# Seven-product matrix stages: GpSimd's sums moved to VectorE and PSUM, and another order of the products

## The chip, the cores and the metric

One core of one Trainium2 chip runs the whole program. The metric is the device time of one execution in microseconds (us); several executions are timed and the median is taken. The engines are TensorE (PE, its weight loads PEld), VectorE (DVE), ScalarE (ACT), GpSimd (POOL) and SyncE (SP), which issues most of the DMAs.

## The reference

512 tokens of width 1024, in float32, go through two programs one behind the other. The first is one block: three branches (dilated attention, a pooling mixer, a state-space scan), gated and added up, a product with `w_o`, and a feed-forward part of width 2816. The second has two layers: three branches (differential attention, retention, grouped-query attention), gated, a product with `w_out`, and an MLP of width 4096. What matters here are the products that come back to width 1024:

```
x = x + merged @ w_o[i]
x = x + conv_ffn(rmsnorm(x, ln2_g[i]), ffn_w_up[i], ffn_conv_w[i], ffn_conv_b[i], ffn_w_down[i])
...
h = h + jnp.einsum('bsd,de->bse', merged, w_out[l])
m = jnp.einsum('bsd,df->bsf', rms_norm(h, mlp_norm[l]), w_mlp_in[l])
m = jnp.square(jax.nn.relu(m))
h = h + jnp.einsum('bsf,fd->bsd', m, w_mlp_out[l])
```

## The kernel before, in words

**Every large product is split.** A float32 operand becomes a high half (ACT's copy, L294) and a low half (DVE's subtraction, L295), and each term of a product is three matmuls (high by high, high by low, low by high). `split` (L293) does that. Weights come raw in DMAs of 512 KB on SP's queue into one of RAWS buffers, and `halve` (L235) splits each 128x1024 piece into `whi` and `wlo`, of which there are HALVES buffers each. Products of the `feat` kind are lines 269 to 271, of the `tok` kind lines 280 to 282.

**`quick` (L928) is the product back to width 1024 by seven block products in place of eight.** Left side and weights are cut into 2x2 blocks. The products of sums of blocks, lines 960 to 962, are added up into the four blocks of X (pages of 128x512). It runs 14 times: once for `w_o`, three times for `ffn_w_down` (8, 8 and 6 pages of 128 features), and in each of the two layers once for `w_out` and four times for `w_mlp_out`, each time right behind the stage that makes the pages of its left side.

**`Forms` (L71) makes the sums of the left blocks.** Each time two new pages r1 and r2 are there, `make` (L85) forms r2 (products 2 and 4), r1 (products 1 and 7), s (products 5 and 6) and w (product 3) from them: three sums of 128x256 on POOL (L89 to L91), one on DVE (L92), and splits each of the four with ACT and DVE. 55 pairs of pages go this way.

**The sums of the weight blocks** are `combine` (L948): eight sums of 128x1024 per run, of which every second is POOL's:

```
def combine(out, x, y, op):
    for j, (o, a, b) in enumerate(zip(out, x, y)):
        engines[j % 2].tensor_tensor(o, a, b, op=op)
```

The products run in the order 1, 5, 3, 6, 2, 7, 4, and the weight blocks are loaded in the order b11, b12, b22, b11 again, b21. Product 1 goes to the PSUM bank pair `a`; ACT copies it out (L998) to the pages `u`, DVE adds product 6 to them (L1019, L1021), and POOL adds `u` to X eight times per run (`add_u`, L973). The other products are added from PSUM to X by DVE (`add`, L967 and L969).

**What sets the order.** Each engine works through its own list of instructions in order. A scheduler makes the lists when the program is built: it places each instruction by its sources' expected times, so that an edit in one place moves others. An instruction that waits holds up all that stand behind it on its engine. Products 1 and 5 are written with their last pair of pages (k = n - 1) left for later (L989 and below), so that matmuls on older pages stand ahead of those that need the pages made last. `gated` (L640) frees its pages `y` at its very end.

Of the kernel before, what the change touches and what calls it, by code (L numbers as in the profile page):

```python
# [12 lines left out]
AF = mybir.ActivationFunctionType  # L13
ALU = mybir.AluOpType
# [10 lines left out]
RAWS = 5  # L25
HALVES = 6
# [44 lines left out]
class Forms:  # L71
# [13 lines left out]
    def make(self, r1, r2):  # L85
        B = self.body
        g, v, c, d = B.nc.gpsimd, B.nc.vector, slice(0, 256), slice(256, 512)
        s, w = B.pgs(2, True)
        g.tensor_tensor(s.t[:, c], r1.t[:, d], r2.t[:, d], op=ALU.add)  # L89
        g.tensor_tensor(s.t[:, d], s.t[:, c], r1.t[:, c], op=ALU.subtract)  # L90
        g.tensor_tensor(w.t[:, c], r2.t[:, c], s.t[:, d], op=ALU.subtract)  # L91
        v.tensor_tensor(r1.t[:, d], r1.t[:, c], r1.t[:, d], op=ALU.subtract)  # L92
        out = []
# [24 lines left out]
class Body:  # L118
# [521 lines left out]
    def gated(self, U, wg, g0, bias, y, wy, kt, acc, first, last, perm=False):  # L640
# [8 lines left out]
        for i in range(8 + AHEAD):  # L649
# [23 lines left out]
            t = T.pop(c)  # L673
            if first:
                a = self.pg()
                acc.append(a)
                nc.vector.scalar_tensor_tensor(a.t, t.t, 1.0, py, op0=ALU.add, op1=ALU.mult)
            else:
                a = acc[c].t
                nc.vector.scalar_tensor_tensor(t.t, t.t, 1.0, py, op0=ALU.add, op1=ALU.mult)  # L680
                (nc.vector if last else nc.gpsimd).tensor_tensor(t.t if last else a, a, t.t, op=ALU.add)
# [6 lines left out]
        self.free(y)  # L688
# [239 lines left out]
    def quick(self, w, k0, kt, F, X, scale=1.0, rows=None, turn=None):  # L928
# [8 lines left out]
        engines = (nc.vector, nc.gpsimd)  # L937
# [10 lines left out]
        def combine(out, x, y, op):  # L948
            for j, (o, a, b) in enumerate(zip(out, x, y)):
                engines[j % 2].tensor_tensor(o, a, b, op=op)  # L950
# [20 lines left out]
        def add_u(t, h, u):  # L971
            x = X[t][h].t
            nc.gpsimd.tensor_tensor(x, x, u.t, op=ALU.add)  # L973

# [15 lines left out]
        u = self.pgs(2)  # L990
# [4 lines left out]
        product(5, W5, d, b=n - 1)  # L995
        product(1, W1, a, a=n - 1)
        for q in two:
            nc.scalar.activation(u[q].t, a[q], AF.Copy, scale=scale)  # L998
            add_u(q, 0, u[q])
        product(5, W5, d, a=n - 1)  # L1000
        b22 = [load(2, 2, j) for j in js]
        W3 = right(b22)
# [3 lines left out]
        combine(b12, b22, b12, ALU.subtract)  # L1006
        b11 = [load(1, 1, j) for j in js]
        combine(b11, b12, b11, ALU.add)
        W6 = right(b11)
        for q in two:  # L1010
            add(q, 1, d[q])
        b = bank()
        product(6, W6, b)
        W7 = right(b12)
        b21 = [load(2, 1, j) for j in js]
        W2 = right(b21)
        for q in two:
            if scale == 1.0:
                nc.vector.tensor_tensor(u[q].t, u[q].t, b[q], op=ALU.add)  # L1019
            else:  # L1020
                nc.vector.scalar_tensor_tensor(u[q].t, b[q], scale, u[q].t, op0=ALU.mult, op1=ALU.add)  # L1021
            add_u(q, 1, u[q])
            sums(q)
        for q in two:
            add_u(2 + q, 1, u[q])
            add_u(2 + q, 0, u[q])
        e = bank()
        product(2, W2, e)
        combine(b21, b21, b11, ALU.subtract)
        for q in two:  # L1030
            add(q, 0, e[q])
            if rows:
                xn[q] = rows(q, ss[q])
        c = bank()
        product(7, W7, c)
        W4 = right(b21)
        for q in two:
            add(2 + q, 1, c[q])
            sums(2 + q)
            if turn:  # L1040
                turn(q, xn[q])
        product(4, W4, c, more=True)
        for q in two:
            add(2 + q, 0, c[q])
            if rows:
                xn[2 + q] = rows(2 + q, ss[2 + q])
        self.free(u, F)
# [730 lines left out]
```

## Time and profile before

| what | value |
|---|---|
| median of 3 runs | 2946.03 us (2943.02 to 2946.54) |
| the profiled execution, its own time | 2942.34 us |
| span in the trace | 2940.2 us |
| mean granted TensorE clock | 0.985 |
| PE busy | 2830.1 us (96%) |
| DVE busy | 2041.5 us (69%) |
| ACT busy | 1307.2 us (44%) |
| POOL busy | 938.3 us (32%) |
| chain that ended last, by engine | PE 76%, DVE 8%, POOL 7%, DMA 4%, ACT 2%, issue 2% |

The profiled execution lies 3.7 us below the median of the runs. Its span is 2.1 us shorter than its own time. Matmuls are pipelined, so one that is shown with 0.39 us starts 0.227 us after the one before it; the distance of two starts is what counts.

### The profile page before, as it was taken

What the parts mean: (1) busy time and instruction counts of PE and PEld (TensorE: products, weight loads), DVE (VectorE), ACT (ScalarE), POOL (GpSimd) and SP (SyncE); (2) the same over time, 40 slices, a digit from 0 to 9 for tenths busy, and PEclk for the clock granted to TensorE, in tenths of its full rate; (3) what the DMA queues carried; (4) which work ended last, traced back from release to release, by engine and by line L of the source; (5) the groups of instructions that cost most, each with busy time, mean ns of one, the idle gap of its engine ahead of it and who ended that gap; (6) DMA issues with size and microseconds to landing.
All of it is one profiled execution on the core that took longest, in us unless ns stands there. A gap on an engine that the chain in (4) does not pass through costs nothing.

```text
span 2940.2 us, 36920 instructions
## 1 busy us (share of the span) xinstructions
PE 2830.1 (96%) x13639; PEld 2361.2 (80%) x13639; DVE 2041.5 (69%) x3316; ACT 1307.2 (44%) x2249; POOL 938.3 (32%) x763
## 2 busy tenths in 40 slices
PE   8999999998999979999999899999999999989999
PEld 7888887887877868888787777787888887778777
DVE  4345477757778786856776787777765766877776
ACT  4344243334444445553464444444554455444443
POOL 0001105314132244211632344345321432534444
PEclk9999999999999989999999999999999999999999
DMA  7243331324242432222222332344222222323341
GB/s 217 82 126 105 100 97 55 88 77 151 74 142 72 133 112 87 88 75 73 73 69 68 118 112 88 101 130 149 84 65 89 64 67 61 122 83 115 115 129 65
DMA packets 225655, 288.20 MB, mean 98 GB/s; under 512 B 17769, under 2 KB 155331, under 8 KB 225475
## 3 DMA queue, kind: packets, MB, share of 16 engines
q1 hardware_dynamic: 212288, 272.77, 30.4%
q10 hardware_dynamic: 13187, 13.08, 1.5%
q8 instruction: 107, 1.75, 0.2%
q14 instruction: 73, 0.60, 0.1%
HBM read 276.30 MB, written 11.67 MB: 98 GB/s over the span
## 4 chain that ended last, share of the span: by engine, by line
PE 76%; DVE 8%; POOL 7%; DMA 4%; ACT 2%; issue 2%; ACTq 0%; SPq 0%; POOLq 0%; DVEq 0%
PE mm L270 14%; PE mm L269 14%; PE mm L271 14%; PE mm L280 4%; PE mm L281 4%; PE mm L282 4%; PE ax L960 4%; PE ax L961 4%; PE ax L962 4%; PE ax L301 3%; DVE wlo L295 3%; POOL raw L950 2%; DMA raw<-in_w_mlp_out_dram 2%; POOL pg L89 1%; DVE pg L295 1%
## 5 line engine op out<-in xcount | busy, mean ns | idle before, releaser
L295 DVE TENSOR_TENSOR wlo<-raw,whi 128x1024 fp32r<-128x1024 f32 (+3 forms) x554 | 730.3, 1325 | 276.6 <-ACT whi L294 269.1
L294 ACT CAST whi<-raw 128x1024 fp32r<-128x1024 f32 (+3 forms) x554 | 565.4, 1031 | 591.3 <-PE mm L270 318.0
L270 PE MATMUL mm<-ul,whi 128*128 128x512 f32 (+1 forms) x1792 | 689.2, 385 | 5.7 <-DVE ul L295 5.7
L269 PE MATMUL mm<-uh,whi 128*128 128x512 f32 (+1 forms) x1792 | 690.8, 387 | 2.0 <-ACT uh L294 2.0
L271 PE MATMUL mm<-uh,wlo 128*128 128x512 f32 (+1 forms) x1792 | 687.4, 384 | 0.0
L270 PEld LDWEIGHTS mm<-ul,whi 128*128 128x128 f32 x1792 | 340.7, 190 | 71.1 <-DVE ul L295 7.0
L269 PEld LDWEIGHTS mm<-uh,whi 128*128 128x128 f32 x1792 | 339.8, 190 | 66.8 <-ACT uh L294 2.9
L271 PEld LDWEIGHTS mm<-uh,wlo 128*128 128x128 f32 x1792 | 340.6, 190 | 64.7 <-issue 0.6
L960 PE MATMUL ax<-whi,pg 128*128 128x512 f32 x770 | 309.6, 406 | 55.2 <-ACT pg L294 43.8
L961 PE MATMUL ax<-wlo,pg 128*128 128x512 f32 x770 | 309.2, 402 | 0.0
L962 PE MATMUL ax<-whi,pg 128*128 128x512 f32 x770 | 298.0, 398 | 0.0
L280 PE MATMUL mm<-whi,uh 128*128 128x512 f32 (+3 forms) x736 | 280.5, 381 | 1.5 <-ACT uh L294 1.5
L281 PE MATMUL mm<-wlo,uh 128*128 128x512 f32 (+3 forms) x736 | 278.1, 378 | 0.0
L282 PE MATMUL mm<-whi,ul 128*128 128x512 f32 (+3 forms) x736 | 278.0, 378 | 0.0
L294 ACT CAST pg<-pg 128x512 fp32r<-128x512 f32 (+2 forms) x264 | 144.9, 574 | 261.8 <-DVE pg L92 66.3
L950 POOL TENSOR_TENSOR raw<-raw,raw 128x1024 f32<-128x1024 f32 (+1 forms) x56 | 159.2, 2843 | 314.7 <-DVE wlo L295 152.4
L973 POOL TENSOR_TENSOR pg<-pg,pg 128x512 f32<-128x512 f32 x112 | 209.6, 1895 | 91.0 <-ACT pg L998 48.5
L295 DVE TENSOR_TENSOR pg<-pg,pg 128x512 fp32r<-128x512 f32 (+2 forms) x264 | 198.1, 776 | 53.3 <-ACT pg L294 51.3
L960 PEld LDWEIGHTS ax<-whi,pg 128*128 128x128 f32 x770 | 149.3, 194 | 98.5 <-ACT pg L294 50.2
L89 POOL TENSOR_TENSOR pg<-pg,pg 128x256 f32<-128x256 f32 x55 | 59.1, 1075 | 421.5 <-DVE pg L1677 163.8
L301 PE MATMUL ax<-c_k_ident,pg 128*128 128x128 f32 x993 | 150.6, 279 | 33.4 <-DVE pg L1146 10.8
L962 PEld LDWEIGHTS ax<-whi,pg 128*128 128x128 f32 x770 | 149.4, 194 | 32.8 <-DVE pg L295 0.4
(264 smaller groups left out, 4387.1 us busy)
## 6 DMA issues: line engine op xcount, KB each, us to landing
raw<-in_w_in_dram SPq DMA_DIRECT2D x180, 512.0 KB, 3.7
raw<-in_w_mlp_out_dram SPq DMA_DIRECT2D x80, 512.0 KB, 3.6
raw<-in_w_mlp_in_dram SPq DMA_DIRECT2D x64, 512.0 KB, 4.3
raw<-in_ffn_w_up_dram SPq DMA_DIRECT2D x44, 512.0 KB, 3.8
raw<-in_ffn_w_down_dram SPq DMA_DIRECT2D x25, 512.0 KB, 3.5
raw<-in_w_out_dram SPq DMA_DIRECT2D x20, 512.0 KB, 3.7
raw<-in_w_branch_dram SPq DMA_DIRECT2D x16, 512.0 KB, 3.9
raw<-in_w_o_dram SPq DMA_DIRECT2D x10, 512.0 KB, 4.3
```

What stands on the lines that cost most here:

```text
L269: mm(ps, hi[:, cols], uh, start=k == 0, stop=False)
L270: mm(ps, hi[:, cols], ul, start=False, stop=False)
L271: mm(ps, lo[:, cols], uh, start=False, stop=k == nk - 1)
L280: mm(ps, uh, hi, start=k == 0, stop=False)
L281: mm(ps, uh, lo, start=False, stop=False)
L282: mm(ps, ul, hi, start=False, stop=k == n - 1)
L294: self.nc.scalar.copy(hi, src)
L295: self.nc.vector.tensor_tensor(lo, src, hi.bitcast(F32), op=ALU.subtract)
L301: self.nc.tensor.transpose(pt[:, i * P:(i + 1) * P], s, self.ident)
L960: mm(ps, uh[:, c], hi, start=not more and k == 0, stop=False, skip_group_check=more)
L961: mm(ps, uh[:, c], lo, start=False, stop=False, skip_group_check=more)
L962: mm(ps, ul[:, c], hi, start=False, stop=k == n - 1, skip_group_check=more)
```

## The change

- **`Forms.make`**: the three sums on POOL are now DVE's. The order is L89 (s's first half), then the difference inside r1 (L90, before L92), then s's second half (L91) and w (L92).
- **`combine`**: all eight sums of a run are DVE's.
- **No pages `u`**: product 6 is accumulated onto product 1 in the PSUM pair `a`, products 7 and 4 onto that; product 3 onto product 5 in the pair `d`; product 2 goes to two banks of the `mm` kind, `e`. ACT's copy (28 in all), DVE's sum with `u` (28) and `add_u` on POOL (112) are gone; DVE's adds from PSUM to X become 14 per run from 12.
- **Order**: products 1, 2, 5, 6, 3, 7, 4; weight blocks b11, b21, b12, b22, b21 again. The first two products are written without their last pair of pages. The number of matmuls and of loads stays.
- **Buffers**: 7 raw ones from 5, 5 pairs of halves from 6 (the same bytes).
- **`gated`** frees its pages `y` ahead of its last addition.

```diff
-RAWS = 5
-HALVES = 6
+RAWS = 7
+HALVES = 5
...
-        g.tensor_tensor(s.t[:, c], r1.t[:, d], r2.t[:, d], op=ALU.add)
-        g.tensor_tensor(s.t[:, d], s.t[:, c], r1.t[:, c], op=ALU.subtract)
-        g.tensor_tensor(w.t[:, c], r2.t[:, c], s.t[:, d], op=ALU.subtract)
+        v.tensor_tensor(s.t[:, c], r1.t[:, d], r2.t[:, d], op=ALU.add)
         v.tensor_tensor(r1.t[:, d], r1.t[:, c], r1.t[:, d], op=ALU.subtract)
+        v.tensor_tensor(s.t[:, d], s.t[:, c], r1.t[:, c], op=ALU.subtract)
+        v.tensor_tensor(w.t[:, c], r2.t[:, c], s.t[:, d], op=ALU.subtract)
...
             t = T.pop(c)
+            if c == 7:
+                self.free(y)
...
-        self.free(y)
...
         def combine(out, x, y, op):
-            for j, (o, a, b) in enumerate(zip(out, x, y)):
-                engines[j % 2].tensor_tensor(o, a, b, op=op)
+            for o, a, b in zip(out, x, y):
+                nc.vector.tensor_tensor(o, a, b, op=op)
...
         product(1, W1, a, b=n - 1)
-        u = self.pgs(2)
+        W2 = right([load(2, 1, j) for j in js])
+        e = [self.mm() for _ in two]
+        product(2, W2, e, b=n - 1)
+        product(1, W1, a, a=n - 1)
+        product(2, W2, e, a=n - 1)
         b12 = [load(1, 2, j) for j in js]
         combine(b11, b12, b11, ALU.subtract)
         W5 = right(b11)
         d = bank()
-        product(5, W5, d, b=n - 1)
-        product(1, W1, a, a=n - 1)
+        product(5, W5, d)
         for q in two:
-            nc.scalar.activation(u[q].t, a[q], AF.Copy, scale=scale)
-            add_u(q, 0, u[q])
-        product(5, W5, d, a=n - 1)
...
+            add(q, 0, a[q])
+        W6, W3 = [], []
+        for j in js:
+            t = load(2, 2, j)
+            combine([b11[j]], [t], [b11[j]], ALU.subtract)
+            W6 += right([b11[j]])
+            combine([b12[j]], [t], [b12[j]], ALU.subtract)
+            W3 += right([t])
+        for q in two:
+            add(q, 0, e[q])
+        product(6, W6, a, more=True)
         for q in two:
             add(2 + q, 1, d[q])
         product(3, W3, d, more=True)
+        for q in two:
+            add(q, 1, a[q])
+        W7 = right(b12)
         for q in two:
             add(q, 1, d[q])
...
+        product(7, W7, a, more=True)
+        b21 = [load(2, 1, j) for j in js]
+        combine(b21, b21, b11, ALU.subtract)
         W4 = right(b21)
         for q in two:
-            add(2 + q, 1, c[q])
+            add(2 + q, 1, a[q])
...
-        product(4, W4, c, more=True)
+        product(4, W4, a, more=True)
         for q in two:
-            add(2 + q, 0, c[q])
+            add(2 + q, 0, a[q])
```

How it moves the lists is shown at the second `w_mlp_out` run of the first layer, which the rows further below show too. Lines behind 680 have other numbers in the changed kernel: 1663 there is 1677 before, the instruction that makes a page of the MLP. In the names, `pg` are pages of 128x512, `raw` the raw weights, `whi` and `wlo` their halves, `ax` and `mm` PSUM banks. First the lists of POOL and of DVE before, from where the last pages come; the last pair r1, r2 is pg1226 and pg1228, and their sum s is pg1229:

```order
L950 TENSOR_TENSOR raw1653_15286<-raw1639_15196,raw1653_15286 128x1024
L89 TENSOR_TENSOR pg1229_15140<-pg1226_15109,pg1228_15138 128x256
L90 TENSOR_TENSOR pg1229_15140<-pg1229_15140,pg1226_15109 128x256
L91 TENSOR_TENSOR pg1230_15141<-pg1228_15138,pg1229_15140 128x256
L973 TENSOR_TENSOR pg1103_13646<-pg1103_13646,pg1237_15192 128x512
L973 TENSOR_TENSOR pg1105_13648<-pg1105_13648,pg1238_15193 128x512
```

```order
L1677 SCALAR_TENSOR_TENSOR pg1228_15138<-mm1629_15111,pg1227_15136 128x512
L295 TENSOR_TENSOR pg1234_15151<-pg1228_15138,pg1233_15150 128x512
L295 TENSOR_TENSOR wlo1655_15291<-raw1652_15284,whi1654_15290 128x1024
L92 TENSOR_TENSOR pg1226_15109<-pg1226_15109 128x256
L295 TENSOR_TENSOR pg1232_15147<-pg1226_15109,pg1231_15146 128x512
L295 TENSOR_TENSOR pg1236_15155<-pg1229_15140,pg1235_15154 128x512
L295 TENSOR_TENSOR pg1224_15067<-pg1230_15141,pg1223_15066 128x256
```

And DVE's list with the change, from the same place; r1 and r2 are pg1214 and pg1216 now, s is pg1217, and raw1644 is the second load of b21:

```order
L295 TENSOR_TENSOR wlo1625_15159<-raw1606_15076,whi1624_15158 128x1024
L1663 SCALAR_TENSOR_TENSOR pg1216_15054<-mm1605_15027,pg1215_15052 128x512
L950 TENSOR_TENSOR raw1606_15076<-raw1630_15194,raw1606_15076 128x1024
L89 TENSOR_TENSOR pg1217_15056<-pg1214_15025,pg1216_15054 128x256
L295 TENSOR_TENSOR pg1222_15067<-pg1216_15054,pg1221_15066 128x512
L950 TENSOR_TENSOR raw1644_15306<-raw1644_15306,raw1606_15076 128x1024
L90 TENSOR_TENSOR pg1214_15025<-pg1214_15025 128x256
L91 TENSOR_TENSOR pg1217_15056<-pg1217_15056,pg1214_15025 128x256
L295 TENSOR_TENSOR wlo1627_15163<-raw1607_15078,whi1626_15162 128x1024
L92 TENSOR_TENSOR pg1218_15057<-pg1216_15054,pg1217_15056 128x256
L295 TENSOR_TENSOR pg1220_15063<-pg1214_15025,pg1219_15062 128x512
```

The difference inside r1 stood behind POOL's sums (it overwrites what L89 reads), and those behind a combine of POOL's; now all stand in one list on DVE, with two combines and two halves of weights between them.

Then PE's list before and with the change, up to the first matmuls that read the pages made last (before: the high half of r1, pg1231; with the change: that of r2, pg1221, in the second piece, and that of r1, pg1219, in the third):

```order
L960 MATMUL ax1645_15209<-whi1642_15204,pg1221_15062 128x512
L961 MATMUL ax1645_15209<-wlo1643_15205,pg1221_15062 128x512
L962 MATMUL ax1645_15209<-whi1642_15204,pg1222_15063 128x512
L960 MATMUL ax1636_15172<-whi1634_15168,pg1231_15146 128x512
L961 MATMUL ax1636_15172<-wlo1635_15169,pg1231_15146 128x512
```

```order
L961 MATMUL mm1621_15121<-wlo1619_15117,pg1207_14974 128x512
L962 MATMUL mm1621_15121<-whi1618_15116,pg1208_14975 128x512
L960 MATMUL mm1620_15120<-whi1618_15116,pg1221_15066 128x512
L961 MATMUL mm1620_15120<-wlo1619_15117,pg1221_15066 128x512
L960 MATMUL mm1621_15121<-whi1618_15116,pg1221_15066 128x512
L961 MATMUL mm1621_15121<-wlo1619_15117,pg1221_15066 128x512
```

```order
L960 MATMUL ax1629_15167<-whi1624_15158,pg1183_14796 128x512
L961 MATMUL ax1629_15167<-wlo1625_15159,pg1183_14796 128x512
L962 MATMUL ax1629_15167<-whi1624_15158,pg1184_14797 128x512
L960 MATMUL ax1612_15088<-whi1610_15084,pg1219_15062 128x512
L961 MATMUL ax1612_15088<-wlo1611_15085,pg1219_15062 128x512
L960 MATMUL ax1613_15089<-whi1610_15084,pg1219_15062 128x512
```

Before, 36 matmuls of products 1 and 5 stand between the last one of the MLP and the first on r1. With the change there are 36 of products 1 and 2 ahead of the first on r2, and 52 ahead of the first on r1; the first of product 6, which adds onto the bank pair `a`, is the 73rd.

## Rows read from the trace of the kernel before

**Rows 1.** The page: busy time of the engines, and the chain that ended last

```profile
PE 2830.1 (96%) x13639; PEld 2361.2 (80%) x13639; DVE 2041.5 (69%) x3316; ACT 1307.2 (44%) x2249; POOL 938.3 (32%) x763
PE 76%; DVE 8%; POOL 7%; DMA 4%; ACT 2%; issue 2%; ACTq 0%; SPq 0%; POOLq 0%; DVEq 0%
```

**Rows 2.** Waits of PE: who for whom, us in total, times, longest us

```profile
PE ax L960 <- ACT pg L294: 43.8, 14, 4.7
PE ax L301 <- DVE pg L1146: 10.8, 1, 10.8
```

**Rows 3.** Groups by line and shape: busy us, mean ns, idle time before them

```profile
L295 DVE TENSOR_TENSOR wlo<-raw,whi 128x1024 fp32r<-128x1024 f32 x521 | 702.3, 1355 | 246.2 <-ACT whi L294 238.7 <-PE ax L301 5.2
L294 ACT CAST whi<-raw 128x1024 fp32r<-128x1024 f32 x521 | 542.7, 1052 | 552.3 <-PE mm L270 292.0 <-PE ax L962 137.1 <-POOL raw L950 49.9
L960 PE MATMUL ax<-whi,pg 128*128 128x512 f32 x770 | 309.6, 406 | 55.2 <-ACT pg L294 43.8 <-DVE pg L967 4.2 <-ACT whi L294 3.4
L973 POOL TENSOR_TENSOR pg<-pg,pg 128x512 f32<-128x512 f32 x112 | 209.6, 1895 | 91.0 <-ACT pg L998 48.5 <-DVE pg L1019 26.7 <-DVE pg L967 14.1
L950 POOL TENSOR_TENSOR raw<-raw,raw 128x1024 f32<-128x1024 f32 x52 | 153.0, 2943 | 281.8 <-DVE wlo L295 133.7 <-DMA raw<-in_w_mlp_out_dram 101.4 <-DMA raw<-in_ffn_w_down_dram 23.3
L950 DVE TENSOR_TENSOR raw<-raw,raw 128x1024 f32<-128x1024 f32 x56 | 83.4, 1490 | 22.1 <-DMA raw<-in_w_mlp_out_dram 14.4 <-DMA raw<-in_w_out_dram 6.4 <-DMA raw<-in_ffn_w_down_dram 0.6
L967 DVE TENSOR_TENSOR pg<-pg,ax 128x512 f32<-128x512 f32 x110 | 73.5, 678 | 25.4 <-PE ax L962 25.4
L89 POOL TENSOR_TENSOR pg<-pg,pg 128x256 f32<-128x256 f32 x55 | 59.1, 1075 | 421.5 <-DVE pg L1677 163.8 <-DVE pg L1119 136.6 <-DVE pg L681 121.1
L90 POOL TENSOR_TENSOR pg<-pg,pg 128x256 f32<-128x256 f32 x55 | 58.7, 1066 | 4.2
```

**Rows 4.** Chain of waits at the second `w_mlp_out` run of layer one: start, us, what

```profile
1805.00 1.24 DVE wlo L295
1806.25 3.47 DMA raw<-in_w_mlp_out_dram
...
1809.85 3.21 POOL raw L950
1813.06 0.69 POOL pg L89
...
1813.78 0.44 DVE pg L92
...
1814.24 0.63 ACT pg L294
```

**Rows 5.** PE's timeline there: start, us, instruction, idle before it

```profile
1812.04 0.39 PE L962 MATMUL ax<-whi,pg 128*128 128x512 f32 x1
1814.91 0.50 PE L960 MATMUL ax<-whi,pg 128*128 128x512 f32 x1 [2.48 <-ACT pg L294]
```

**Rows 6.** Stretches: length, busy us of PE, PEld, DVE, ACT, POOL, granted clock, DMA

```profile
1049.00:1106.00 57.00, 39.84 (x151) 31.72 (x150) 49.17 (x75) 30.72 (x61) 26.19 (x20) 0.79 0.45 136
1610.00:1664.00 54.00, 45.85 (x195) 36.83 (x193) 45.45 (x49) 26.98 (x42) 32.35 (x19) 0.94 0.50 160
1804.00:1851.00 47.00, 44.52 (x190) 36.25 (x189) 34.32 (x35) 19.59 (x24) 23.05 (x13) 0.96 0.44 135
1851.00:1890.00 39.00, 39.00 (x174) 32.31 (x173) 27.45 (x33) 16.96 (x27) 14.31 (x11) 1.00 0.29 81
2528.00:2580.00 52.00, 45.41 (x192) 36.64 (x190) 42.94 (x46) 24.60 (x38) 32.10 (x19) 0.93 0.54 167
```

**Rows 7.** Lines 950 and 92 alone: duration ns min/median/max

```profile
L950 DVE TENSOR_TENSOR raw<-raw,raw x56: 1210/1225/2201, 654.1 to 2916.8; 128x1024 f32<-128x1024 f32 x56
L950 POOL TENSOR_TENSOR raw<-raw,raw x56: 1298/2533/5649, 656.9 to 2921.9; 128x1024 f32<-128x1024 f32 x52, 128x512 f32<-128x512 f32 x4
L92 DVE TENSOR_TENSOR pg<-pg x55: 410/426/965, 620.2 to 2903.2; 128x256 f32<-128x256 f32 x55
```

**Rows 8.** DVE's timeline there: one low half of 128x1024

```profile
1809.60 1.22 DVE L295 TENSOR_TENSOR wlo<-raw,whi 128x1024 fp32r<-128x1024 f32 x1 [0.26 <-ACT whi L294]
```

More of the change, by code (lines that the diff above doesn't have):

```diff
@@ L86, in make @@
         B = self.body
-        g, v, c, d = B.nc.gpsimd, B.nc.vector, slice(0, 256), slice(256, 512)
+        v, c, d = B.nc.vector, slice(0, 256), slice(256, 512)
         s, w = B.pgs(2, True)
-        g.tensor_tensor(s.t[:, c], r1.t[:, d], r2.t[:, d], op=ALU.add)
-        g.tensor_tensor(s.t[:, d], s.t[:, c], r1.t[:, c], op=ALU.subtract)
-        g.tensor_tensor(w.t[:, c], r2.t[:, c], s.t[:, d], op=ALU.subtract)
+        v.tensor_tensor(s.t[:, c], r1.t[:, d], r2.t[:, d], op=ALU.add)
         v.tensor_tensor(r1.t[:, d], r1.t[:, c], r1.t[:, d], op=ALU.subtract)
+        v.tensor_tensor(s.t[:, d], s.t[:, c], r1.t[:, c], op=ALU.subtract)
+        v.tensor_tensor(w.t[:, c], r2.t[:, c], s.t[:, d], op=ALU.subtract)
         out = []
@@ L936, in quick @@
         parts = [(a, min(a + 2, n)) for a in range(0, n, 2)]
-        engines = (nc.vector, nc.gpsimd)
         def load(e, h, j):
@@ L969, in add @@
                 nc.vector.scalar_tensor_tensor(x, y, scale, x, op0=ALU.mult, op1=ALU.add)
-        def add_u(t, h, u):
-            x = X[t][h].t
-            nc.gpsimd.tensor_tensor(x, x, u.t, op=ALU.add)
         ss, xn = {}, {}
@@ L994, in quick @@
         d = bank()
-        product(5, W5, d, b=n - 1)
-        product(1, W1, a, a=n - 1)
+        product(5, W5, d)
         for q in two:
-            nc.scalar.activation(u[q].t, a[q], AF.Copy, scale=scale)
-            add_u(q, 0, u[q])
-        product(5, W5, d, a=n - 1)
-        b22 = [load(2, 2, j) for j in js]
-        W3 = right(b22)
+            add(q, 0, a[q])
[9 more added lines that the diff above has]
+        product(6, W6, a, more=True)
         for q in two:
@@ L1005, in quick @@
         product(3, W3, d, more=True)
[L1006 to L1009, printed above, removed]
+        for q in two:
+            add(q, 1, a[q])
+        W7 = right(b12)
         for q in two:
             add(q, 1, d[q])
[L1012 to L1022, printed above, removed]
-            sums(q)
[L1024 to L1031, printed above, removed]
+            sums(q)
             if rows:
                 xn[q] = rows(q, ss[q])
-        c = bank()
-        product(7, W7, c)
+        product(7, W7, a, more=True)
+        b21 = [load(2, 1, j) for j in js]
+        combine(b21, b21, b11, ALU.subtract)
         W4 = right(b21)
         for q in two:
-            add(2 + q, 1, c[q])
+            add(2 + q, 1, a[q])
             sums(2 + q)
@@ L1041, in quick @@
                 turn(q, xn[q])
-        product(4, W4, c, more=True)
+        product(4, W4, a, more=True)
         for q in two:
-            add(2 + q, 0, c[q])
+            add(2 + q, 0, a[q])
             if rows:
                 xn[2 + q] = rows(2 + q, ss[2 + q])
-        self.free(u, F)
+        self.free(F)
         return lambda: [turn(t, xn[t]) for t in (2, 3)] if turn else None
```

## The prediction

> **What bounds the kernel now.** Start with the page's busy times and the chain that ended last [rows 1]. PE is busy 2830.1 of 2940.2 us and stands for 76% of the chain. The change leaves every matmul where it is in number and size, so it can give back two things only: time in which PE stands idle, and time in which its clock is granted at the lower of its levels. DVE is busy 2041.5 us and POOL 938.3, and the chain goes through them for 8% and 7%: in some places they are late for PE. Where, PE's waits say [rows 2]. The largest entry is L960, the first of the three matmuls of `quick`, waiting for ACT's high halves of the left blocks: 43.8 us in 14 times, the longest 4.7, and there are 14 runs of `quick`. The group of L960 adds bank and weight waits and comes to 55.2 us idle [rows 3]. The other large single wait, 10.8 us at L301, is for L1146, a row scaling behind the last `ffn_w_down` run that no edit touches; it stays.
>
> Follow one of the fourteen. In the chain at the second `w_mlp_out` run [rows 4] DVE splits a weight piece (1.24), its raw buffer comes free, a load of 3.47 us fills it, POOL's L950 takes 3.21 on what has landed, then come POOL's L89, DVE's L92 and ACT's cast, and only then PE. The three sums of the last pair of pages stand behind a POOL sum of weights that itself waits for a DMA. On PE's timeline [rows 5] the last covered matmul starts at 1812.04, the next at 1814.91: 2.48 us idle. A matmul takes 0.224 us here, 39.00 us for 174 in the stretch behind [rows 6]. So the 36 covering matmuls last 8.1 us, the MLP's last matmul ended at 1812.27 - 8.1 = 1804.2 (called E below), and r1's high half came at E + 10.7.
>
> Then the clock. In the stretches around such waits the granted clock is 0.96, 0.94 or 0.79 of 2.4 GHz, in the stretch between two runs 1.00 [rows 6]: behind an idle PE some matmuls run at 1.2 GHz. One `w_mlp_out` run loses 0.04 x 47 = 1.9 us so, the first `w_out` run 0.06 x 54 = 3.2.
>
> **The change part by part.**
>
> The three sums of `Forms` go from POOL (1.08 and 1.07 us each for L89 and L90 [rows 3]) to DVE, which takes 0.43 for that shape [rows 7]: 165 x 0.43 = 71 us of DVE. The 52 sums of `combine` that POOL did in 2.94 us each [rows 3] cost DVE 1.22 each [rows 7], four half-sized ones about 0.7: 66 us. DVE's adds from PSUM become 28 more, its sums with `u` 28 fewer, at 0.68 each [rows 3]: nothing. So DVE gets 137 us more to do. Against that stands what POOL cost DVE: a low half takes 1355 ns on average [rows 3] and 1.22 alone [rows 8], so 521 x 0.13 = 70 us come back if POOL's sums are what stretched them; POOL loses its L973 (209.6), its L950 (159) and L89 to L91. DVE would end near 2110 busy. None of this is on PE's path by itself; what counts is when each piece is ready.
>
> Is DVE full there? In the stretch of the second `w_mlp_out` run it is busy 34.32 of 47 us, in the one behind 27.45 of 39 [rows 6]: about 70%, and the change adds some 5 us of `combine` and 5 of `Forms` to such a pair of 86 us, less what comes back. That fits. The Trainium skill, in "Perfetto Trace Analysis", section "Optimizing Scalar/DVE Operations", speaks against the change: where DVE is saturated, giving work to GpSimd can make sense, though it adds that a read port which the two share may spoil that. By the rule, in a stage in which DVE is full, each of the moved sums would lengthen the stage; the 70% say that none is full as a whole, so the sum below goes by the order of the list.
>
> Now the order, at the place that front of the change shows, again from E. DVE's last page instruction starts at about E + 2.3: with five pairs of halves the first half of W5 needs the pair that the MLP's last matmul reads, so a cast (1.05 [rows 3]) and a low half (1.22 [rows 8]) stand ahead of it. Then the list says: page 0.68, sum of weights 1.22, L89 0.43, low half of r2 0.68, sum of weights 1.22, L90 0.43, and r1 is ready for ACT, whose cast takes 0.63 [rows 4]: E + 2.3 + 4.7 + 0.6 = E + 7.6. Its low half follows at E + 9.7 (0.43 + 1.22 + 0.43 + 0.68 more up to its end). r1 is first due behind 52 matmuls, E + 11.6; before it came at E + 10.7 and was due at E + 8.1. The next due date is that of product 6, which writes into the bank pair `a` only after DVE has added it to X. DVE's list up to the second of these adds holds six pieces of 1.22, six of 0.68 and five of 0.43, together 13.6: E + 15.9, due at 72 x 0.224 = E + 16.1. So the wait of 2.48 goes, and what is late next is that add, by about nothing. I charge 0.7 us per `w_mlp_out` run, 5.6 in all.
>
> In the other six runs I have no such slack. Two `ffn_w_down` runs are fed by a stage in which DVE also does a convolution; I charge 2 us each. The third has three pairs of pages, so a quarter less cover: 4.5. The runs of `w_o` and the two of `w_out` have rows to normalise at their end, and DVE is busy 45.45 of 54 us in such a stretch [rows 6]: 3 each. Together 17.5.
>
> Loads: as many as before, but b21's second one now feeds a sum that stands on DVE ahead of r1. It goes into the raw buffer that the second low half of W2 frees, in time for a landing near E + 3.2 (3.47 us each [rows 4]), and is asked for at E + 5.3. No charge. Between nothing and the 6.3 us that POOL's L950 waits for such a load on average (101.4 us in 16 times; in the total of [rows 3]) I take nothing, since two more raw buffers let it start earlier.
>
> One pair of halves fewer: ACT's casts already wait 292 us for the `feat` matmuls to free one [rows 3], yet PE waits for a high half of weights only 3.4 us [rows 3]; bounds nothing and another 3.4, I take nothing. The earlier freeing of `y`, the copies of `u` on ACT and the two banks of the `mm` kind touch nothing that PE waits for: nothing. Product 6's adds onto product 1 need no other matmuls.
>
> Sum. Up for recovery are 55.2 us of idle time and the half clock behind it: some 1.8 us in eight stretches like the one at 1804 and 3.2 in each `w_out` run make 21, of which I count 20; the 0.21 x 57 = 12 of the stretch at 1049 belong mostly to the wait for L1146. 75.2 less 5.6 and 17.5 is 52. The profiled execution took 2942.3; less 52 is 2890, and 3.7 more for the median of the runs, which lies so far above it, is **2894**.
>
> **The rivals.**
>
> *DVE's list waits for loads* (slower). DVE takes its instructions in order. POOL could wait for a load with nothing but sums behind it; on DVE the same wait holds up r1, s, the adds that free the banks, and the low halves. DVE's own L950 already waits for loads, 14.4 us and 6.4 [rows 3]. If the load of b21 came as late as POOL's did, 6.3 us per run, then 14 x 6.3 = 88 us of idle time and 14 x 1.9 = 27 us of half clock would stand in place of the 75: 2986. It decides from 75 / 14 = 5.4 us per run (with the clock, about 3.7 idle). For it: the sum on raw1644 does stand ahead of L90. Against it: the buffer is free 2 us before it must be. 0.1.
>
> *The wait only moves* (small gain). If DVE's pieces keep their stretched 1.36 us in place of 1.22 and a load is now and then late, the add to `a` comes 1.5 us late, and W5, W6 and W3 behind it: some 3 us per run with the clock, 42 us, and the 10 more of the shorter and slower runs: 75 - 52 = 23 gained, 2923. For it: the add's slack of 0.2 us. Against it: with POOL nearly silent the two-input sums should take their shortest times, 1210 and 410 ns [rows 7]. 0.18. At the end of this case lies one without any gain, each wait as long as before, near 2946: 0.06.
>
> *More than forecast.* All waits of L960 go with their clock: 2942.3 - 75 + 3.7 = 2871. 0.08.
>
> *The change does not do what it says*: that matmuls onto a bank that already holds a sum run slower than onto a fresh one. The rows exclude most of it: products 3 and 4 are added on top of 5 and 7 already, and L960 to L962 keep their pace there. Under 0.02, within the slow case.
>
> **How the numbers follow.** Forecast 0.58, more 0.08, wait moved 0.18, none 0.06, slower 0.1. The range reaches from 2871, where all waits are gone, to 2930, a little over the case in which the wait moves: it leaves out half of the first tail, the case of none, and the slow one, about 0.2. A change of 0.2%, 5.9 us, is about what a measurement of this kernel can tell from none. Faster by more takes the forecast, the larger gain and the moved wait, 0.84; within 0.2% lie 0.06, slower 0.1.
>
> **What would show it.** Right: L960's idle time under 25 us, no wait of L960 for ACT's `pg` over 1.5 us in the `w_mlp_out` runs, low halves near 1.24 us on average, L950 on DVE 108 times at 1.22 to 1.3, POOL busy near 400, DVE near 2110, a granted clock near 0.99, and the 10.8 us at L301 still there. Wrong: DVE's L950 idle for over 50 us behind DMAs (the slow case), or L960 waiting 2 to 3 us for L967 or for `whi` 14 times (the wait moved). If the idle time goes and the median does not fall, the idle time was not what set the end.

## The result

The changed kernel takes 2862.81 us in the median of 4 runs (2860.07 to 2864.98), the kernel before 2944.53 (2940.38 to 2946.54, 4 runs): a ratio of 0.9724, 95% interval 0.9707 to 0.9741. That is 81.7 us less. 2894 was forecast, with a range down to 2871: the direction was right, the size was not, and the range did not hold it. The profiled execution of the changed kernel took 2862.31 us with a span of 2860.5, so the two spans to compare are 2940.2 and 2860.5, 79.7 us apart.

The page of the changed kernel, busy times and the chain that ended last, answers to [rows 1]:

```profile
PE 2800.2 (98%) x13639; PEld 2339.8 (82%) x13639; DVE 2026.8 (71%) x3565; ACT 1300.3 (45%) x2221; POOL 408.9 (14%) x430
PE 86%; DVE 6%; POOL 3%; DMA 2%; issue 1%; ACT 1%; ACTq 0%; SPq 0%; DVEq 0%; POOLq 0%
```

PE runs the same 13639 matmuls. Its idle time was 2940.2 - 2830.1 = 110.1 us and is 2860.5 - 2800.2 = 60.3: 49.8 us less. Its busy time fell by 29.9 us with the same matmuls, while the mean granted clock rose from 0.985 to 0.996: over the span, 44 us of clock were not granted before, and 11 are not now. 49.8 + 29.9 = 79.7. POOL lost over half of its work, and DVE, which took over sums of some 137 us by the forecast's estimate, is busy 15 us *less* than before.

PE's waits with the change (who for whom, us in total, times, longest) answer to [rows 2]. L1132 is L1146 before, the row scaling behind the last `ffn_w_down` run:

```profile
PE ax L301 <- DVE pg L1132: 11.1, 1, 11.1
...
PE ax L960 <- DVE pg L967: 4.1, 4, 1.3
...
PE ax L960 <- DVE pg L969: 2.7, 2, 1.3
PE ax L960 <- ACT pg L294: 1.4, 1, 1.4
...
PE ax L962 <- DVE pg L295: 1.0, 3, 0.4
PE mm L962 <- DVE pg L295: 0.6, 1, 0.6
```

The 43.8 us of waits for the high halves of the left blocks are down to 1.4 in one place. What is left before lines 960 to 962 adds up to 4.1 + 2.7 + 1.4 + 1.0 + 0.6 = 9.8, against 55.2 before [rows 3]. Most of it is the wait for a bank that DVE must first add to X (L967 and L969, L969 in the runs with a scale, those of `w_o` and `w_out`). As forecast, it is that add which is late next, and the 11 us at L301 are still there.

The groups by line and shape answer to [rows 3]:

```profile
L295 DVE TENSOR_TENSOR wlo<-raw,whi 128x1024 fp32r<-128x1024 f32 x521 | 643.3, 1240 | 289.0 <-ACT whi L294 286.7 <-PE po L1603 0.5
L960 PE MATMUL ax<-whi,pg 128*128 128x512 f32 x660 | 253.8, 392 | 8.2 <-DVE pg L967 4.1 <-DVE pg L969 2.7 <-ACT pg L294 1.4
L950 DVE TENSOR_TENSOR raw<-raw,raw 128x1024 f32<-128x1024 f32 x108 | 131.2, 1217 | 5.0 <-DMA raw<-in_w_o_dram 1.7 <-DMA raw<-in_w_mlp_out_dram 1.2 <-DMA raw<-in_w_out_dram 1.1
L967 DVE TENSOR_TENSOR pg<-pg,ax 128x512 f32<-128x512 f32 x132 | 87.9, 680 | 35.2 <-PE ax L962 34.9
L89 DVE TENSOR_TENSOR pg<-pg,pg 128x256 f32<-128x256 f32 x55 | 23.1, 420 | 0.7
```

The low halves average 1240 ns, the sums of weights 1217 where DVE had needed 1490 and POOL 2943, and the waits for loads in front of them are 5.0 us in all. The slow rival, in which DVE's list stands behind late loads, did not come about.

And the stretches: length, busy us of PE, PEld, DVE, ACT, POOL, granted clock, DMA share, GB/s. Of the changed kernel first, then the same two stretches around the end of the feed-forward part before:

```profile
1037.00:1070.00 33.00, 29.56 (x126) 22.88 (x125) 32.65 (x52) 20.47 (x38) 1.46 (x2) 1.00 0.54 156
1070.00:1100.00 30.00, 18.94 (x93) 15.78 (x92) 20.64 (x50) 17.10 (x35) 8.36 (x10) 0.83 0.38 140
1590.00:1637.00 47.00, 44.15 (x201) 35.75 (x200) 45.11 (x63) 26.21 (x41) 2.73 (x3) 1.00 0.62 189
1768.00:1811.00 43.00, 43.00 (x191) 35.63 (x190) 32.85 (x41) 18.11 (x20) 0.00 (x0) 1.00 0.48 147
```

```profile
1049.00:1089.00 40.00, 33.63 (x127) 26.48 (x126) 37.00 (x45) 21.18 (x40) 23.53 (x15) 0.87 0.42 125
1089.00:1120.00 31.00, 20.21 (x95) 16.95 (x94) 20.13 (x51) 17.20 (x35) 7.25 (x10) 0.78 0.39 132
```

The second `w_mlp_out` run (1768) has PE busy for all of its 43 us at full clock, with POOL not used at all. The `w_out` run at 1590 has its clock back too. Of the 12 us of clock that the stretch at 1049 to 1106 lost before, 0.13 x 40 = 5.2 lay ahead of the wait for L1146, and are gone.

### The profile page after: what moved, and what is told of

Read it like the earlier page. It is cut to its first block, busy times and chain, and to the rows that moved or that the text cites. A ratio compares the mean times of both kernels' runs of the same rounds, so it can differ in the third digit from the quotient of the medians.

```text
span 2860.5 us, 36576 instructions
## 1 busy us (share of the span) xinstructions
PE 2800.2 (98%) x13639; PEld 2339.8 (82%) x13639; DVE 2026.8 (71%) x3565; ACT 1300.3 (45%) x2221; POOL 408.9 (14%) x430
## 4 chain that ended last, share of the span: by engine, by line
PE 86%; DVE 6%; POOL 3%; DMA 2%; issue 1%; ACT 1%; ACTq 0%; SPq 0%; DVEq 0%; POOLq 0%
PE mm L270 16%; PE mm L269 16%; PE mm L271 16%; PE ax L960 4%; PE ax L961 4%; PE ax L962 4%; PE mm L280 4%; PE mm L282 4%; PE mm L281 4%; PE ax L301 3%; DVE wlo L295 2%; PE po L1603 1%; PE po L1345 1%; PE ax L1250 1%; PE ax L1249 1%
## 5 line engine op out<-in xcount | busy, mean ns | idle before, releaser
L295 DVE TENSOR_TENSOR wlo<-raw,whi 128x1024 fp32r<-128x1024 f32 (+3 forms) x554 | 668.6, 1213 | 314.7 <-ACT whi L294 308.6
L309 POOL TENSOR_TENSOR stats<-stats,mhalf 128x1 f32<-128x1 f32 (+3 forms) x84 | 95.1, 1134 | 1193.5 <-DVE stats L329 673.2
L960 PE MATMUL ax<-whi,pg 128*128 128x512 f32 x660 | 253.8, 392 | 8.2 <-DVE pg L967 4.1
L961 PE MATMUL ax<-wlo,pg 128*128 128x512 f32 x660 | 255.8, 390 | 0.0
L962 PE MATMUL ax<-whi,pg 128*128 128x512 f32 x660 | 252.8, 391 | 1.1 <-DVE pg L295 1.0
L301 PE MATMUL ax<-c_k_ident,pg 128*128 128x128 f32 x993 | 151.3, 278 | 30.6 <-DVE pg L1132 11.1
L301 PEld LDWEIGHTS ax<-c_k_ident,pg 128*128 128x128 f32 x993 | 123.4, 144 | 55.7 <-POOL pg L1214 11.5
L295 DVE TENSOR_TENSOR pg<-pg,pg 128x512 fp32r<-128x512 f32 (+2 forms) x264 | 160.6, 630 | 5.4 <-ACT pg L294 4.8
L280 PEld LDWEIGHTS mm<-whi,uh 128*128 128x128 f32 x736 | 138.7, 188 | 24.1 <-issue 1.0
L281 PEld LDWEIGHTS mm<-wlo,uh 128*128 128x128 f32 x736 | 138.8, 189 | 23.5 <-DVE wlo L295 1.1
L282 PEld LDWEIGHTS mm<-whi,ul 128*128 128x128 f32 x736 | 138.5, 188 | 23.5 <-DVE ul L295 1.3
```

The source lines that it names most:

```text
L280: mm(ps, uh, hi, start=k == 0, stop=False)
L281: mm(ps, uh, lo, start=False, stop=False)
L282: mm(ps, ul, hi, start=False, stop=k == n - 1)
L295: self.nc.vector.tensor_tensor(lo, src, hi.bitcast(F32), op=ALU.subtract)
L301: self.nc.tensor.transpose(pt[:, i * P:(i + 1) * P], s, self.ident)
L960: mm(ps, uh[:, c], hi, start=not more and k == 0, stop=False, skip_group_check=more)
```

## The experiments

Twelve kernels were run, four at a time on one chip, each beside the kernel before, whose median was 2942.95 to 2944.61 in these sessions and in that of the result. So differences of 2 to 3 us between two kernels of different sessions tell nothing. Theory A: where the sums are made sets the waits. Theory B: the longer cover does, 52 matmuls on older pages in place of 36. Theory C: DVE is faster when POOL does not read beside it. Later ones: D, the raw buffers; E, the path through the pages `u`.

**Both kinds of sums back on POOL.** `Forms.make` as before, and in `combine`:

```diff
-            for o, a, b in zip(out, x, y):
-                nc.vector.tensor_tensor(o, a, b, op=op)
+            for j, (o, a, b) in enumerate(zip(out, x, y)):
+                engines[(j0 + j) % 2].tensor_tensor(o, a, b, op=op)
```

`j0` goes on counting where the changed kernel sums one piece at a time, so that every second sum is POOL's again.

> The changed kernel with the three sums of Forms and every second sum of weight blocks put back on GpSimd; the new order of products, the sums in PSUM and the buffers stay. Theory A (where the sums are made sets the wait): r1's high half comes some 10.7 us after the last matmul of the stage ahead, as before, and later weight sums stand behind it on GpSimd too; L960 idles 25 to 45 us and the time is 2895 to 2925. Theory B (the longer cover of 52 matmuls, 11.6 us, is enough by itself): L960 idles under 15 us, the time is 2865 to 2885.

Measured: 2882.39 (ratio 0.9797, interval 0.9782 to 0.9811). L961 (L960 in the changed kernel) idles 10.3 us and L963 10.2, the latter for low halves of the left blocks. The time and the first of these waits are as B had them: with the cover, or with whatever else the change brings, most of the gain survives POOL's sums.

**Only the sums moved, in the kernel before.** The same edits the other way round.

> The kernel before with only the sums of Forms and of the weight blocks moved to VectorE; products 1, 5, 3, 6, 2, 7, 4, the pages u and GpSimd's eight additions per run stay. Theory A: the first wait of each run shrinks from 3.3 us to under 1, L960 idles 10 to 20 us, the time is 2870 to 2890. Theory B: with a cover of 36 matmuls (8.1 us) r1 is still late by 1 to 2 us; L960 idles 30 to 45 us, the time is 2900 to 2925.

Measured: 2899.91 (0.9856, 0.9841 to 0.9871), 44 us less than before, over half of the gain. DVE is busy 2088.0 us in it, 46.5 more than before. PE's waits in this kernel, where L959 is the first of the three matmuls and L966 the add from PSUM:

```profile
PE ax L959 <- ACT pg L294: 16.4, 7, 3.9
...
PE ax L959 <- DVE pg L966: 6.2, 2, 5.7
```

The first wait is gone in six of the eight `w_mlp_out` runs and stands at 1.0 us in two; in the `ffn_w_down` and `w_out` runs it is still 1.5 to 3.9 us. The time lies on the lower edge of B's range; the idle time of L959, 28.8 us in all, lies between the two. So A holds for the `w_mlp_out` runs, and not for the others.

**The old cover in the changed kernel.**

```diff
         product(1, W1, a, b=n - 1)
-        W2 = right([load(2, 1, j) for j in js])
-        e = [self.mm() for _ in two]
-        product(2, W2, e, b=n - 1)
-        product(1, W1, a, a=n - 1)
-        product(2, W2, e, a=n - 1)
         b12 = [load(1, 2, j) for j in js]
         combine(b11, b12, b11, ALU.subtract)
         W5 = right(b11)
         d = bank()
-        product(5, W5, d)
+        product(5, W5, d, b=n - 1)
+        product(1, W1, a, a=n - 1)
+        product(5, W5, d, a=n - 1)
+        W2 = right([load(2, 1, j) for j in js])
+        e = [self.mm() for _ in two]
+        product(2, W2, e)
```

> The changed kernel with the products in the order 1, 5, 2, 6, 3, 7, 4 and the blocks b12 loaded ahead of b21, so that the matmuls on older pages are again those of products 1 and 5 and a sum of weights stands ahead of them. Theory A: within 0.3% of the changed kernel, 2860 to 2871. Theory B: a first wait of 1 to 3 us comes back in most of the 14 runs, 2880 to 2910.

Measured: 2864.05 (0.9735, 0.9719 to 0.9751), the changed kernel's time within its spread. B falls: with the rest of the change in place the longer cover is worth nothing measurable. No wait of L960 for ACT's `pg` is left with the old cover either. My own estimate had said it: r1 at E + 7.6, due at E + 8.1 with 36 matmuls. Whether the longer cover pays where the sums are POOL's was not tried.

**As much work on POOL as the additions of u were, read by nobody.**

```diff
+        zz = self.pg()
...
         product(6, W6, a, more=True)
+        for i in range(8):
+            nc.gpsimd.tensor_tensor(zz.t, F.pages[-1 - i % 4].t.bitcast(F32), F.pages[-1].t.bitcast(F32), op=ALU.add)
...
-        self.free(F)
+        self.free(zz, F)
```

> The changed kernel with eight additions of 128x512 per run on GpSimd that nobody reads (two pages of the left blocks into a spare page, from product 6 on): as much GpSimd work as the additions of u that were taken away. Theory C (the gain beyond my forecast is VectorE's, freed of GpSimd's reads): low halves rise from 1.24 us on average to 1.3 or more, L960 idles 15 to 30 us, 2872 to 2890. Theory A or B alone: VectorE slows but PE does not notice, 2860 to 2868.

Measured: 2878.98 (0.9786, 0.9772 to 0.9801), 16 us above the changed kernel and within C's range. Groups by line in this kernel:

```profile
L295 DVE TENSOR_TENSOR wlo<-raw,whi 128x1024 fp32r<-128x1024 f32 x521 | 672.8, 1296 | 270.1 <-ACT whi L294 267.8 <-PE po L1606 0.5
L960 PE MATMUL ax<-whi,pg 128*128 128x512 f32 x660 | 256.9, 396 | 17.2 <-DVE pg L967 8.8 <-DVE pg L969 5.5 <-ACT pg L294 1.4
L967 DVE TENSOR_TENSOR pg<-pg,ax 128x512 f32<-128x512 f32 x132 | 87.5, 678 | 34.3 <-PE ax L962 34.1
```

The low halves, with two inputs from SBUF, go from 1240 to 1296 ns; the add with one input from PSUM stays at 678. What PE waits for is that add all the same; it stands behind the stretched ones in DVE's list. PE does not wait everywhere. The stretches of the `w_o` run and of the second `w_mlp_out` run, and the `w_o` run of the changed kernel, with the columns of before:

```profile
671.00:715.00 44.00, 41.22 (x181) 33.72 (x180) 42.12 (x51) 22.35 (x35) 16.91 (x10) 0.96 0.52 167
1783.00:1825.00 42.00, 42.00 (x187) 34.79 (x186) 34.63 (x40) 17.59 (x20) 16.39 (x8) 1.00 0.48 151
```

```profile
669.00:709.00 40.00, 40.00 (x186) 33.22 (x184) 37.89 (x51) 23.13 (x36) 1.63 (x2) 1.00 0.59 194
```

In the second, with 16.39 us of POOL work beside it, PE loses nothing; in the first, where DVE was busy 37.89 of 40 us without that work, it loses 2.8 us. The reading is limited in one way: the extra additions also hold the pages of the left blocks a little longer, and a kernel without that was not tried.

**The buffers of before in the changed kernel** (`RAWS = 5`, `HALVES = 6`).

> The changed kernel with 5 raw buffers and 6 pairs of halves, as before. Theory D (the two more raw buffers carry the stages of ffn_w_down, w_o and w_out, since VectorE's sums of weights no longer wait for a load there): VectorE's L950 idles 10 us or more behind loads, L960 waits 1 to 3 us in these six runs, 2870 to 2885. If the buffers are worth nothing: within 0.2% of the changed kernel, 2858 to 2868.

Measured: 2874.79 (0.9769, 0.9755 to 0.9784), within D's range. The sums of weights wait for loads as D has it:

```profile
L950 DVE TENSOR_TENSOR raw<-raw,raw 128x1024 f32<-128x1024 f32 x108 | 130.9, 1222 | 27.9 <-DMA raw<-in_w_mlp_out_dram 13.6 <-DMA raw<-in_ffn_w_down_dram 5.4 <-DMA raw<-in_w_out_dram 4.8
```

27.9 us in place of 5.0. But L960 idles 10.0 us there against 8.2, so most of the 12 us does not sit where D put it. Against the changed kernel's trace, the time from a run's start to the next run's start is 13.2 us longer over the five runs that end with the normalisation of rows (`w_o`, the last `ffn_w_down`, the two of `w_out`, the last `w_mlp_out` of the first layer), and 2.0 us shorter over the other nine together. What in these five stretches hangs on the buffers was not taken apart.

**The buffers of the change, added to the kernel before with its sums on DVE.**

> The kernel before with the sums of Forms and of the weight blocks on VectorE and with 7 raw buffers and 5 pairs of halves; the pages u, GpSimd's additions and the old order of products stay. Theory D: the first waits of the ffn_w_down and w_out runs (1.7 to 4.1 us with 5 buffers) shrink to under 1 us, and 2899.9 becomes 2872 to 2885; what is left to 2863 is then the adding of u. If the buffers are worth nothing: 2895 to 2904, and the sums in PSUM carry the rest.

Measured: 2902.32 (0.9855, 0.9839 to 0.9872): no gain over 2899.91, and D falls as the cause of what the second run lacks against the changed kernel. The waits of L949 for loads did go, from 14.8 to 2.7 us; the time did not follow. The buffers made a difference only beside the rest of the change.

**One kind of sum back at a time**, `Forms` first, then `combine`.

> The changed kernel with only the three sums of Forms back on GpSimd, 55 times. With both kinds of sums back the time was 2882.4. If the sums of Forms carry that difference, since they stand on the way to the pages that PE needs first: 2874 to 2882. If the sums of weights do, since GpSimd's 2.84 us pieces stretch VectorE's: 2863 to 2869.

> The changed kernel with only every second sum of weight blocks back on GpSimd, 56 times. If the sums of Forms carry the 19.6 us of both together: 2863 to 2869. If the sums of weights do: 2874 to 2882, low halves at 1.28 us or more on average, and the waits in the ffn_w_down runs.

Measured: 2865.67 (0.9737, 0.9722 to 0.9751) with the sums of `Forms` on POOL, 2871.39 (0.9755, 0.974 to 0.9769) with those of `combine`: 2.9 and 8.6 us above the changed kernel, 19.6 with both. The first is where it was expected if the sums of weights carry the difference, and no more than a measurement can tell from nothing; the second lies between its two cases. So the sums of weights carry more, but the two together cost more than the two single costs added up. That either kind alone still fits in part into DVE's slack would explain it, and is not shown. The groups by line with `combine` on POOL, where L951 is L950:

```profile
L295 DVE TENSOR_TENSOR wlo<-raw,whi 128x1024 fp32r<-128x1024 f32 x521 | 690.2, 1330 | 291.2 <-ACT whi L294 289.1 <-PE po L1604 0.5
L961 PE MATMUL ax<-whi,pg 128*128 128x512 f32 x660 | 253.7, 393 | 16.8 <-DVE pg L970 11.5 <-DVE pg L968 4.8 <-DVE stats L329 0.4
L951 POOL TENSOR_TENSOR raw<-raw,raw 128x1024 f32<-128x1024 f32 x52 | 167.3, 3217 | 934.8 <-DVE wlo L295 827.1 <-DMA raw<-in_w_mlp_out_dram 51.8 <-DMA raw<-in_ffn_w_down_dram 21.3
```

Its low halves take 1330 ns, and 11.5 us of its waits are one add in each of the two `w_out` runs (L970, L969 in the changed kernel). The `w_mlp_out` runs lose nothing here either.

**The additions of u on DVE too**, in the kernel of the sixth run.

```diff
-            nc.gpsimd.tensor_tensor(x, x, u.t, op=ALU.add)
+            nc.vector.tensor_tensor(x, x, u.t, op=ALU.add)
```

> The kernel of the sixth run (before, with the sums on VectorE, 7 raw buffers, 5 pairs of halves: 2902.3) with its eight additions of u per run moved from GpSimd to VectorE as well. GpSimd then does nothing for these stages, but the path through u stays: ACT's copy, the sum with product 6, eight additions. Theory C (GpSimd's reads stretch VectorE): low halves fall from 1.34 to 1.24 us, the time to 2880 to 2893. Theory E (the path through u itself is too long, and VectorE has 76 us more to do): 2898 to 2915. By Theory C the rest to 2864, which the changed kernel has with the same order of the first products, is then the path through u.

Measured: 2900.76 (0.9858, 0.9837 to 0.9879), against 2902.32: E. The low halves are back at 1241 ns from 1337, so POOL's reads are out of it, and nothing is won. DVE now has the additions themselves to do; that they use up what the shorter low halves give is the likely reason, not a measured one. From here to the third run, with the same sums on DVE, the same buffers and the same first two products, are 36.7 us, and what differs is `u`: ACT's copy, DVE's sum with product 6 and the eight additions against accumulation in PSUM, with the order of the later products, sums and loads, and the earlier freeing of `y` in `gated`. No run separates these. Between the first start of `quick` and the end the two traces lie 36.2 us apart, and 27.7 of these fall between a run's start and the next one where the run ends with the normalisation of rows (`w_o`, the last `ffn_w_down`, the two of `w_out`, the last `w_mlp_out` of the first layer). In four of these five (not in that of `ffn_w_down`) PE in the third run does the first eight transposes of the rows (L301) ahead of the last matmuls of the run; in the ninth run it does none there. The end of the `w_out` run of the first layer, first with the additions of `u` on DVE, then in the third run:

```profile
1647.17 0.39 PE L961 MATMUL ax<-whi,pg 128*128 128x512 f32 x1
1647.40 1.64 PE L301 MATMUL ax<-c_k_ident,pg 128*128 128x128 f32 x12
```

```profile
1630.80 1.03 PE L301 MATMUL ax<-c_k_ident,pg 128*128 128x128 f32 x8
...
1634.19 0.39 PE L962 MATMUL ax<-whi,pg 128*128 128x512 f32 x1
1634.42 1.15 PE L301 MATMUL ax<-c_k_ident,pg 128*128 128x128 f32 x8
```

The last matmul of the run starts at 1647.17 and at 1634.19. So in the third run the first rows of X were complete by 1630.80, before the run's end. Which part of the bundle does this was not taken apart.

**Towards a faster one.** The wait of 11.1 us at L301 stands behind four small loads for `diff_lam`, which are moved ahead of the second `ffn_w_down` run (`lam` holds the lines of `diff_proj` that load them and work out `nlam`); the cover is chosen by the kind of run, the new one for `w_mlp_out`; then both.

```diff
+            if ip == 1:
+                self.nlam = [self.lam(l) for l in range(2)]
...
-        nlam = self.cp.tile([P, 1], F32, tag="nlam", name=self.nm("nlam"), bufs=1)
+        nlam = self.nlam[l]
...
+        if w.shape[0] == 4096:
+            ...
+        else:
+            ...
```

> The changed kernel with the four small loads of diff_lam of both layers and what is worked out from them moved ahead of the second ffn_w_down run. In the changed kernel VectorE waits 4.67 us for these loads while L1132, which TensorE waits for, stands behind them. If that load ends the wait of 11.1 us at L301: it falls to 5 to 7 us, and with the clock behind it the time is 2853 to 2859. If the normalisation of the rows ends it anyway: 2860 to 2866.

> The changed kernel with the old cover (products 1, 5, 2, ...) in the six runs of w_o, w_out and ffn_w_down and the new one in the eight of w_mlp_out. By the stages of the third run, w_out takes 42.3 us with the old cover and 44.1 with the new one, w_mlp_out 42.0 and 41.6. If these add up: 2856 to 2861. If the gain of one stage is lost in the next: 2861 to 2866.

> Both of the edits before in one kernel: the cover by the kind of run, and the loads of diff_lam early. If they are independent: 2848 to 2856. If the wait at L301 is the same one that the old cover shortens (11.1 us became 5.3 in the third run): 2854 to 2860.

Measured: 2859.92 (2858.38 to 2860.97), 2865.88 (2864.55 to 2869.05) and 2859.81 (2858.26 to 2860.32); ratios 0.9718, 0.9737 and 0.9717. The wait at L301 fell to 6.1 us with the early loads, as expected, but the time by 2.9 us, too little to be told from the changed kernel's 2862.81; it lies between the two cases. Two instructions of POOL for the normalisation end it now, in the chain of that kernel:

```profile
1073.78 1.21 DVE wlo L295
1074.99 0.14 DVE stats L1129 x2
1075.12 0.01 issue
1075.13 2.66 POOL stats L309 x2
...
1077.98 0.67 DVE pg L1134
```

The mixed cover wins nothing, alone or with the early loads, and both times the second of its two cases came about: what the stages of the third run gave singly is lost elsewhere. No version here beats the changed kernel by more than a measurement can tell.

## Why the prediction was wrong

**The step that failed.** The forecast took 52.1 us off the trace's time, and the two traces lie 79.7 apart: 27.6 were missing. That PE's waits and its clock are what can be won was right, and three terms of the sum were mis-sized: the charges for waits that stay (23.1, where 9.8 us were measured), the clock (20, where 29.9 came back) and idle time away from lines 960 to 962 (nothing, where 4.4 went). Behind them stands a judgement that the runs refute: that beyond the moved sums and the longer cover the change brings nothing. The copies of `u`, the `mm` banks and the freeing of `y` were said to touch nothing that PE waits for, and the raw buffers were only a reason for charging no loads. The sums on DVE alone gave 44 us (second run), not far from the 52.1 of the forecast; nearly all of the rest came with what was costed at nothing.

**What bounds the kernel, right.** The gain came out of PE's idle time and of its busy time, that is, its clock: 49.8 + 29.9.

**The order of the list, right and a little better than estimated.** DVE's timeline at the second `w_mlp_out` run of layer one with the change, where E, the start of the first L960, is 1768.5:

```profile
1769.56 1.23 DVE L295 TENSOR_TENSOR wlo<-raw,whi 128x1024 fp32r<-128x1024 f32 x1 [1.54 <-ACT whi L294]
1770.71 0.68 DVE L1663 SCALAR_TENSOR_TENSOR pg<-mm,pg 128x512 f32<-128x512 f32 x1
1771.31 1.21 DVE L950 TENSOR_TENSOR raw<-raw,raw 128x1024 f32<-128x1024 f32 x1
1772.44 0.41 DVE L89 TENSOR_TENSOR pg<-pg,pg 128x256 f32<-128x256 f32 x1
1772.78 0.68 DVE L295 TENSOR_TENSOR pg<-pg,pg 128x512 fp32r<-128x512 f32 x1
1773.38 1.22 DVE L950 TENSOR_TENSOR raw<-raw,raw 128x1024 f32<-128x1024 f32 x1
1774.52 0.41 DVE L90 TENSOR_TENSOR pg<-pg 128x256 f32<-128x256 f32 x1
...
1780.47 1.21 DVE L295 TENSOR_TENSOR wlo<-raw,whi 128x1024 fp32r<-128x1024 f32 x1
1782.48 1.28 DVE L967 TENSOR_TENSOR pg<-pg,ax 128x512 f32<-128x512 f32 x2 [0.80 <-PE ax L962]
```

The page instruction starts at E + 2.2 (2.3 estimated), L90 ends at E + 6.4 (7.0 estimated), and the two adds that free the banks begin at E + 14.0, after 0.80 us in which DVE waited for *PE* to finish product 1. They end at E + 15.3, where the estimate had 15.9. What was off here: I added durations. A piece of 1.21 to 1.23 us starts its successor 1.14 us after its own start, one of 0.68 after 0.60, so the list of 13.6 us takes 12.3. With that, the 0.7 us per `w_mlp_out` run were no charge at all: 5.6 forecast, nothing measured.

**The charges for the other six runs, too high.** 17.5 were forecast. The `ffn_w_down` runs leave 4.1 + 1.4 + 1.0 + 0.6 = 7.1 of waits (8.5 charged), near enough; `w_o` and the two of `w_out` leave 2.7 us (9 charged). That charge rested on no list, only on DVE's busy share, 45.45 of 54 us; the changed kernel has 45.11 of 47 in that stretch, and PE runs on. A high share does not make an engine late. Together, charges of 23.1 stood where 9.8 were due: 13.3 of the 27.6 us by which the gain was short.

**The clock, too low.** I counted 20 us; PE's busy time fell by 29.9. I had put the whole loss of the stretch at 1049 down to the wait for L1146, which stays; its first 40 us held 5.2 that went, and behind the wait the granted clock rose from 0.78 to 0.83. The others come from places outside the stretches I had listed: behind the `w_o` run the clock rose from 0.98 to 1.00, behind the second `w_out` run from 0.94 to 1.00. That is 9.9 of the 27.6.

**Idle time elsewhere, not counted.** 49.8 - (55.2 - 9.8) = 4.4 us: mostly transposes behind the `w_o` and `w_out` runs that waited for X, in a row of PE's waits before that I left out of the sum:

```profile
PE ax L301 <- DVE pg L969: 4.6, 4, 1.2
```

The three, 13.3 + 9.9 + 4.4, add up to the 27.6 us. The end of the range failed with them: 2871 was called the case in which all is recovered, but it was made from the same 55.2 and 20, and so was no bound. A bound from the page would have been PE's idle time over the whole span, 110.1 us, and its lost clock, (1 - 0.985) x 2940.2 = 44 us; I had looked at half of each.

**Which part carries it.** My working leaned on two things, the sums on DVE and the longer cover. The first holds: it makes 44 us alone. The second is worth nothing measurable beside the rest (third run). What I had costed at nothing is worth nearly as much as the first: 36.7 us from the ninth to the third run, where the path through `u` ends, the later order changes and `y` is freed earlier, all at once. The buffers are worth 12 us in the changed kernel and nothing in the kernel before with its sums on DVE (sixth run).

**DVE's load, wrong.** I took its adds from PSUM to be 12 per run before. They are 10 (L967 and L969: 110 + 30 in 14 runs); the sums with `u` are the other two, and I subtracted them again. So DVE got 28 adds more than I charged, 19 us on top of the 137. It ended at 2026.8 in place of the forecast 2110 all the same, so 137 + 19 + 15 = 171 us came back and not 70: the low halves of the weights gave 702.3 - 643.3 = 59, those of the left blocks' 128x512 pages 162.3 - 129.4 = 33, the 56 sums of weights that were DVE's already 15, the difference inside r1 37.1 - 23.1 = 14, and the rest is spread. The 70 had a condition, that POOL's sums are what stretched the low halves. The second run speaks against it: with the sums gone from POOL and the additions of `u` still there, a low half took 1334 ns in place of 1355. Either kind of work is enough, since POOL's sums of weights alone give 1330 in the eighth run.

The rule in the Trainium skill that was weighed ("Perfetto Trace Analysis", section "Optimizing Scalar/DVE Operations") speaks of giving work to GpSimd where DVE is saturated, with the doubt that a shared read port may spoil it. The runs side with the doubt in the main: taking back sums of some 137 us loaded DVE by 46.5 us (2088.0 in the second run, 2041.5 before), and with the additions of `u` gone from POOL as well DVE has less to do than before.

## What to carry to other kernels

Where an engine's list holds work that another engine waits for, add the starts, not the durations, and charge a stage only from its list, never from a busy share. Taking work back from an engine that reads beside another can cost that other less than the work's own time: here 46.5 us for some 137. Test the parts of a change together and singly: here the parts put back one at a time cost 1 (the cover), 3 (the sums of `Forms`), 9 (those of the weights) and 12 us (the buffers), of which the first two cannot be told from nothing, while both kinds of sums alone, moved in the kernel before, made 44. Make the outer bound from the whole span's idle time and clock, not from the rows of the sum.

## What the runs showed of the hardware that was not expected

A DVE instruction with two inputs in SBUF stretched beside POOL (low halves 1239 to 1241 ns on average in the kernels without POOL work in these stages, 1245 to 1355 in those with it, single sums of weights up to 2.77 us beside POOL's), one with an input in PSUM did not: the add to X (L967 and its like) took 677 to 682 ns on average in every kernel. Within one trace it is the same: before, 326 low halves had no instruction of POOL beside them and took 1.22 us on average, none over 1.23; the 195 that had one took 1.58. Of the adds, the 50 that lay wholly beside POOL took 677 ns, the 50 without it 679. POOL pays more: its sums of weights took 2.84 us on average in the first run and 3.22 in the eighth, and 1.28 at the least.

Short waits cost PE a good half as much again in clock: 49.8 us of idle time less came with 29.9 us less of busy time, with the same matmuls and a mean granted clock of 0.996 in place of 0.985.
